# A transformer block on one core: seven-product pairs in all ten groups of the first feed-forward product

## The chip, the cores and the metric

The kernel runs on one core of one Trainium2 chip. The metric is the device time of one execution in microseconds (us). TensorE (PE) multiplies, VectorE (DVE) and ScalarE (ACT) work on tiles, GpSimd (POOL) and SyncE (SP) mostly issue DMA transfers.

## The reference

One block on 256 tokens of width 2048: a gated delta rule branch and a sparse attention branch are gated and merged, then follow layer norm 1 (its result is `x1`), a gated feed-forward layer of inner width 5632, and layer norm 2. The change is in the feed-forward layer, in the gates ahead of it and in how `x1` and the inner activations are kept:

```python
x1 = layer_norm(ALPHA * x + merged @ w_out, ln1_g, ln1_b)
g, u = split(x1 @ w_ffn_in)              # [256, 2048] x [2048, 2 * 5632]
h = silu(g) * u                          # [256, 5632]
out = layer_norm(ALPHA * x1 + h @ w_ffn_out, ln2_g, ln2_b)
```

## The kernel before, in words

**Numbers.** All is fp32. Each operand is split into a high and a low part that PE can multiply at full rate, and a product is three matmuls (`mm3`): high by high, high by low, low by high. Weights come from memory in chunks of 128x1024 (512 KB) on SP's queue; for each, ACT casts `hi` and DVE subtracts `lo` (`chunk`). Tokens are two blocks of 128.

**Pairs.** The large products run over pairs of contraction tiles (256 rows). A *plain pair* (`plain_pair`) is eight products, 24 matmuls of 128x512. A *seven-product pair* (`seven_pair`) gets the same sums from seven products, 21 matmuls, in the manner of Strassen. For it DVE makes sums of weight tiles (`wt`), which are split as well (`thi`, `tlo`), and it needs sums of the left operand, the *forms* (`f_form` for x1; for the inner activations they are written to memory as `d_g` and read back as `gt`). It has a second set of four PSUM banks (`wbank`, as against `bank`), which `sums_chain` adds up after the last such pair. The two sets come from two pools, `acc` and `aux`, of four banks each, which change roles from group to group. The tiles of a pair have names with a prefix by stage: `g_` in the gates, `f_` in the first feed-forward product, none in the second.

**Stages.** Gates (`gate_group` 0 to 3, with the block `wbb` between the first two and the last two and `wba` behind), merge, `wo`, layer norm 1, then the first feed-forward product: group 0 in two plain blocks (`h_chain`), then ten groups of eight pairs (`x_group`, i = 1 to 10), each 512 columns of g and of u. The table `FQ` says which pairs of a group are seven-product ones. After a group, `hidden_chain` makes silu(g) * u, transposes it on PE, splits it into `hH[i]`, `hL[i]` and, where the output product wants forms, writes these to `d_g`. The output product (`group`) has two groups of 22 pairs; pair 2i and 2i+1 read `hH[i]`, `hL[i]`, and `WQ` lists its seven-product pairs.

**Order.** PE and SP follow the program's order as written. DVE, ACT and POOL are ordered by a scheduler with priorities. Side work is written as generators (*chains*), which go on at *ticks*; a tick follows each 12 matmuls (half a pair), and `yield 4` waits four ticks.

**Memory on the chip.** The tiles for `f_wraw`, `f_wt`, `f_thi`, `f_tlo` lie in the places of `hH[7]` to `hH[10]` and `hL[7]` to `hL[10]`, and the forms in the place of `x1`, which is written out to `d_x1` by POOL and read back at i = 8.

Of the kernel before, what the change touches and what calls it, by code (L numbers as in the profile page):

```python
# [34 lines left out]
X1T_WAIT = ((5, 1, 1, 1), (6, 1, 2, 2))  # L35
INV_WAIT = 6
VT_WAIT = 6
WQ = ((2, 4, 6, 8, 9, 11, 13, 14, 16, 18, 19), (3, 5, 7, 8, 10, 12, 13, 15))

GQ = ((4, 6), (2, 4, 6), (2, 4, 6), (2, 4, 6))  # L40
WALL = sorted({*WQ[0], *WQ[1]})
FQ = {1: (4, 6), 2: (4, 6), 3: (3, 4, 6), 4: (4, 6), 5: (3, 4, 6), 6: (4, 6), 7: (3, 4, 6)}

LN2_LOAD = (5, 7, 9, 11)
HELD = 4
N_WARM = 9

# [5 lines left out]
def block_kernel(ctx: ExitStack, tc: tile.TileContext, xT, x, cpack, onehot, relb, convw, alog, dtb, gnw,  # L53
# [13 lines left out]
    def ps_acc():  # L67
        return acc.tile([P, 512], F32, name="acc", tag="acc")
# [20 lines left out]
    def start(gen, at_once=False):  # L89
        chains.append([gen, clock[0] + (next(gen) if at_once else 0)])  # L90
# [20 lines left out]
    def finish():  # L111
        while chains:
            tick()
# [49 lines left out]
            nc.tensor.matmul(ps, xh, lv[:, kk], start=False, stop=False)  # L163
            nc.tensor.matmul(ps, xl, hv[:, kk], start=False, stop=(k == 2 * n - 1))  # L164

    def block_xs(srcs, lh, ll):
        pss = [ps_acc(), ps_acc()]
        for ci, src in enumerate(srcs):
            hi, lo = chunk(src)
            for tb in range(NTB):  # L170
                xs_mm(pss[tb], hi, lo, ci, len(srcs), lh, ll, tb)
            tick()
        return pss
# [262 lines left out]
    def v4(a):  # L436
        return a.rearrange("p (h j) -> p h j", h=4)
# [529 lines left out]
        gate_group(gb, i)  # L967
    for j in range(4):
        js = slice(j * 512, (j + 1) * 512)
        for tb, ps in enumerate(block_xs([wbb[j, k] for k in range(4)], oh_, ol_)):  # L970
            nc.vector.tensor_mul(gb[tb][:, js], ps, gb[tb][:, js])  # L971
    event("bb")
    for i in range(2):
# [21 lines left out]
    hH, hL = [], []

    def h_tiles(pool, n):
        for _ in range(n):
            i = len(hH)
            hH.append(pool.tile([P, 4, S], F32R, name=f"hH{i}", tag=f"hH{i}"))  # L1000
            hL.append(pool.tile([P, 4, S], F32R, name=f"hL{i}", tag=f"hL{i}"))

    h_tiles(hp_, 5)
# [53 lines left out]
    def x1T_chain(tb):  # L1057
        for j in range(4):
            yield X1T_WAIT[tb][j]
            with tc.high_priority(offset=3 * LEAD):  # L1060
                transposed_split(x1, j, tb)
        nc.gpsimd.dma_start(d_x1[tb], x1[tb])
        if tb:
            event("x1")

# [9 lines left out]

    fp = xs_.enter_context(tc.tile_pool(name="fp", bufs=1, side="right", reuse_waits="tile"))

    for tag, shape, dtype, n in (("v", [P, 512], F32, 4), ("hq", [P, 512], F32, 1), ("fg", [P, 2, 4, P], F32, 1),
                                 ("gs", [P, 2, 2, 4, P], F32R, 1)):
        fp.tile(shape, dtype, name=tag, tag=tag, bufs=n)  # L1080

    def fv():
        return fp.tile([P, 512], F32, name="v", tag="v", bufs=4)
# [8 lines left out]
    def h_chain(j, tb, sg, ps):  # L1092
        yield 2
        a = ps()
        for i in range(2):
            nc.tensor.transpose(a[:, i * P:(i + 1) * P], sg[:, i, :], ident)
        ts = slice(tb * P, tb * P + P)
        fs = slice(2 * j, 2 * j + 2)
        split(hH[0][:, fs, ts], hL[0][:, fs, ts], a[:, :2 * P].rearrange("p (k t) -> p k t", k=2))

    block_xs_stag([wfi[0, k] for k in range(8)], xh, xl, ex,
                  lambda tb, ps: start(h_chain(0, tb, gated(tb, ps), ps_aux)))
    l1.close()
# [14 lines left out]

    def f_forms_chain():
        yield "x1"  # L1120
        t = [rp.tile([P, 2, 2, 4, P], F32R, name="f_form", tag=f"x1_{tb}") for tb in range(NTB)]
        for i, q in enumerate((4, 6, 3)):
            yield 1
            f_form[q] = t[i // 2][:, i % 2, 0], t[i // 2][:, i % 2, 1]
            x_form(q, f_form[q], fv(), fv())
# [6 lines left out]

    def hidden_chain(i, bank, v, std):

        if v is None:
            v = [fv() for _ in range(4)]
            for tb in range(NTB):
                nc.scalar.activation(v[2 * tb], bank[2 * tb], AF.Silu)
                nc.vector.tensor_mul(v[2 * tb + 1], bank[2 * tb + 1], v[2 * tb])
        else:  # L1140
            for tb in range(NTB):
                g, u = v[2 * tb:2 * tb + 2]
                nc.vector.tensor_tensor(g, bank[2 * tb], g, op=OP.subtract if tb else OP.add)
                nc.scalar.activation(g, g, AF.Silu)
                nc.vector.tensor_add(u, bank[2 * tb + 1], u)
            for tb in range(NTB):
                g, u = v[2 * tb:2 * tb + 2]
                nc.vector.tensor_mul(u, u, g)
        yield 4 if i < NG else 2
        a = [quad(lambda o, f: nc.tensor.transpose(o, v[2 * tb + 1][:, f * P:(f + 1) * P], ident), std)  # L1150
             for tb in range(NTB)]
        ps = [p for p in (2 * i, 2 * i + 1) if p in WALL]
        if ps:
            hq = fp.tile([P, 512], F32, name="hq", tag="hq", bufs=1)
            nc.scalar.copy(hq, a[1])
        for tb in range(NTB):
            ts = slice(tb * P, tb * P + P)
            split(hH[i][:, :, ts], hL[i][:, :, ts], v4(a[tb]))
        if ps:
            def pv(t, j):  # L1160
                t = t.rearrange("p (q two t) -> p q two t", two=2, t=P)
                return t[:, slice(ps[0] % 2, ps[-1] % 2 + 1), j]
            n = len(ps)
            g = fp.tile([P, 2, 4, P], F32, name="fg", tag="fg", bufs=1)[:, :n]
            gi = [g[:, :, j] for j in range(4)]
            forms(gi, pv(a[0], 0), pv(hq, 0), pv(a[0], 1), pv(hq, 1))
            gs = fp.tile([P, 2, 2, 4, P], F32R, name="gs", tag="gs", bufs=1)[:, :n]
            split(gs[:, :, 0], gs[:, :, 1], g)
            for j, p in enumerate(ps):
                nc.gpsimd.dma_start(d_g[WALL.index(p)], gs[:, j].rearrange("p a b t -> p (a b t)").bitcast(F32))  # L1170

    NG = FT // 4 - 1
    for i in range(1, NG + 1):
        if i > 7:
            h_tiles(hp2, 1)
        if i == 8:
            x1 = [rp.tile([P, D], F32, name=f"x1_{tb}", tag=f"x1_{tb}") for tb in range(NTB)]
            for tb in range(NTB):
                nc.gpsimd.dma_start(x1[tb], d_x1[tb])
        std, shared = (ps_aux, ps_acc) if i % 2 else (ps_acc, ps_aux)  # L1180
        sums = []

        def places():
            sums.extend(fv() for _ in range(4))
            return sums

        bank = x_group(wfg[i - 1], FQ.get(i, ()), std, shared, f_form, fhome, places)
        start(hidden_chain(i, bank, sums or None, std), at_once=True)
    h_tiles(hp2, 1)
    hh_, hl_ = KV(hH), KV(hL)  # L1190


# [147 lines left out]
def _arrays(i):  # L1340
# [13 lines left out]
    def paired(m):  # L1354
# [63 lines left out]
```

## Time and profile before

| | |
|---|---|
| three runs | 1476.67, 1478.28, 1478.88 us |
| median | 1478.28 us |
| profiled execution, its own time | 1477.79 us |
| its span in the profile | 1476.0 us |
| granted PE clock, mean | 0.998 of full |
| busy: PE, DVE, ACT, POOL | 1459.3, 1146.1, 766.5, 52.6 us |

The span goes from the first to the last instruction of the trace; the execution's own time holds what lies around it as well. Busy times are sums over an engine's instructions, so an engine can be busy for 78% of the span and still be the one that is waited for in some stage.

### The profile page before, as it was taken

To read this page: it belongs to the slowest core of one execution; us is meant where nothing else is said; L and a number is where in the kernel's file an instruction comes from. 1 tells how busy PE (TensorE), PEld (TensorE's weight loads), DVE (VectorE), ACT (ScalarE), POOL (GpSimd) and SP (SyncE) were. 2 spreads that over 40 slices of the span, in tenths; PEclk is the share of its full clock that TensorE was granted. 3 is DMA by queue.
4 is the path that set the end of the run, shared out by engine and by line. 5 is a ranking of instruction groups with operands and counts; after the bars stand their busy time and mean duration, and the time that the engine had idled before them with its cause. 6 is when DMAs were issued, how large, how long until landed. Compare 5 with 4: busy or idle time off the path is not lost.

```text
span 1476.0 us, 19311 instructions
## 1 busy us (share of the span) xinstructions
PE 1459.3 (99%) x7191; PEld 1226.0 (83%) x7191; DVE 1146.1 (78%) x1534; ACT 766.5 (52%) x932; POOL 52.6 (4%) x63
## 2 busy tenths in 40 slices
PE   9999999999999999999999999999999999999996
PEld 9888888888888888888878888888888888888885
DVE  6798985468488678776676889988895556999896
ACT  6765443446466456543445556555554444664560
POOL 0001010020010000000000000000000000000000
PEclk9999999999999999999999999999999999999999
DMA  8656584545556665558656566666676666877862
GB/s 295 193 153 198 179 193 152 158 129 158 168 185 215 199 213 187 186 185 299 227 187 207 184 234 216 218 216 236 227 255 220 200 209 224 303 262 244 322 217 87
DMA packets 92398, 307.59 MB, mean 208 GB/s; under 512 B 16448, under 2 KB 17512, under 8 KB 91280
## 3 DMA queue, kind: packets, MB, share of 16 engines
q1 hardware_dynamic: 80592, 283.36, 58.9%
q0 software_dynamic: 4672, 20.65, 4.0%
q10 hardware_dynamic: 7040, 2.36, 0.7%
q8 instruction: 56, 0.92, 0.3%
q14 instruction: 38, 0.31, 0.1%
HBM read 292.50 MB, written 13.83 MB: 208 GB/s over the span
## 4 chain that ended last, share of the span: by engine, by line
PE 95%; DVE 2%; DMA 1%; ACT 1%; issue 1%; SPq 0%; POOLq 0%; DVEq 0%; ACTq 0%
PE acc L142 10%; PE acc L205 10%; PE acc L206 10%; PE acc L204 10%; PE aux L205 8%; PE aux L206 8%; PE aux L204 8%; PE acc L164 7%; PE acc L163 7%; PE acc L162 7%; PE acc L145 5%; PE aux L669 1%; DMA raw<-in_win_dram 1%; DVE lo L82 1%; ACT hi L80 1%
## 5 line engine op out<-in xcount | busy, mean ns | idle before, releaser
L82 DVE TENSOR_TENSOR lo<-raw,hi 128x1024 fp32r<-128x1024 f32 (+1 forms) x421 | 514.8, 1228 | 240.2 <-ACT hi L80 237.1
L80 ACT CAST hi<-raw 128x1024 fp32r<-128x1024 f32 (+1 forms) x421 | 437.7, 1046 | 483.6 <-PE acc L164 125.3
L142 PE MATMUL acc<-X,hi 128*128 128x512 f32 x640 | 203.7, 400 | 0.0
L204 PE MATMUL acc<-hi,X 128*128 128x512 f32 x388 | 151.6, 391 | 0.5 <-DVE s_vT L971 0.5
L206 PE MATMUL acc<-hi,X 128*128 128x512 f32 x388 | 151.0, 389 | 0.0
L205 PE MATMUL acc<-lo,X 128*128 128x512 f32 x388 | 151.0, 389 | 0.0
L145 PEld LDWEIGHTS acc<-X,lo 128*128 128x128 f32 x640 | 120.2, 188 | 28.3
L204 PE MATMUL aux<-hi,X 128*128 128x512 f32 x340 | 132.9, 391 | 0.0
L206 PE MATMUL aux<-hi,X 128*128 128x512 f32 x340 | 132.4, 389 | 0.0
L205 PE MATMUL aux<-lo,X 128*128 128x512 f32 x340 | 132.3, 389 | 0.0
L162 PE MATMUL acc<-hi,X 128*128 128x512 f32 x320 | 127.1, 397 | 0.0
L145 PE MATMUL acc<-X,lo 128*128 128x256 f32 x640 | 126.0, 278 | 0.0
L164 PE MATMUL acc<-hi,X 128*128 128x512 f32 x320 | 124.7, 390 | 0.0
L163 PE MATMUL acc<-lo,X 128*128 128x512 f32 x320 | 124.6, 389 | 0.0
L142 PEld LDWEIGHTS acc<-X,hi 128*128 128x128 f32 x640 | 97.5, 189 | 2.0 <-ACT hi L80 0.7
L204 PEld LDWEIGHTS acc<-hi,X 128*128 128x128 f32 x388 | 72.8, 188 | 15.9 <-DVE s_vT L971 1.0
L206 PEld LDWEIGHTS acc<-hi,X 128*128 128x128 f32 x388 | 72.8, 188 | 15.1
L205 PEld LDWEIGHTS acc<-lo,X 128*128 128x128 f32 x388 | 72.9, 188 | 15.0
L206 PEld LDWEIGHTS aux<-hi,X 128*128 128x128 f32 x340 | 63.8, 188 | 13.3
L205 PEld LDWEIGHTS aux<-lo,X 128*128 128x128 f32 x340 | 63.8, 188 | 13.1
L204 PEld LDWEIGHTS aux<-hi,X 128*128 128x128 f32 x340 | 63.8, 188 | 13.0
L164 PEld LDWEIGHTS acc<-hi,X 128*128 128x128 f32 x320 | 60.1, 188 | 12.7
(518 smaller groups left out, 2562.6 us busy)
## 6 DMA issues: line engine op xcount, KB each, us to landing
raw<-in_wfg_dram SPq DMA_DIRECT2D x143, 512.0 KB, 4.0
raw<-in_wws_dram SPq DMA_DIRECT2D x80, 512.0 KB, 3.8
raw<-in_wfo_dram SPq DMA_DIRECT2D x69, 512.0 KB, 4.6
raw<-in_wgt_dram SPq DMA_DIRECT2D x53, 512.0 KB, 3.6
raw<-in_win_dram SPq DMA_DIRECT2D x37, 512.0 KB, 3.7
raw<-in_wo_dram SPq DMA_DIRECT2D x32, 512.0 KB, 4.3
wraw<-in_wfo_dram SPq DMA_DIRECT2D x19, 512.0 KB, 5.0
gt<-d_g SPq DMA_DIRECT2D x19, 512.0 KB, 6.6
```

Source lines behind the costliest of these rows:

```text
L80: nc.scalar.copy(hi, raw)
L82: nc.vector.tensor_sub(lo, raw, hi.bitcast(F32))
L142: nc.tensor.matmul(pss[c], hv[:, kk, cs[c]], X2[k // 4][:, k % 4], start=(k == 0), stop=False, skip_group_check=True)
L145: nc.tensor.matmul(pss[c][:, :S], lv[:, kk, cs[c]], xh[:, k, :], start=False, stop=(k == KT - 1), skip_group_check=True)
L162: nc.tensor.matmul(ps, xh, hv[:, kk], start=(k == 0), stop=False)
L163: nc.tensor.matmul(ps, xh, lv[:, kk], start=False, stop=False)
L164: nc.tensor.matmul(ps, xl, hv[:, kk], start=False, stop=(k == 2 * n - 1))
L204: nc.tensor.matmul(o, sh, hi, start=first, stop=False)
L205: nc.tensor.matmul(o, sh, lo, start=False, stop=False)
L206: nc.tensor.matmul(o, sl, hi, start=False, stop=last)
L669: nc.tensor.matmul(o, l, r, start=True, stop=True)
```

## The change

- `FQ`: before, groups 1 to 7 had two or three seven-product pairs (17 in all) and 8 to 10 had none. Now group 1 has (4, 6) and the nine others (2, 4, 6), 29 in all.
- `WQ`: 18 instead of 19 seven-product pairs in the output product.
- `hidden_chain`: the transposes come after three ticks in every group (before: four, and two in the last). Both transposed tiles are copied by ACT into `v` tiles (`hq`), and the splits and forms read the copies.
- To free places, the inner activations of group 0 and of groups 1 and 2 go to *passing tiles* (in the place of `hH0`, `hL0`) and are written to memory by POOL (`put_out`, `d_h`). They become positions 8, 9 and 10 of the output product and are read back one by one by SP in its group 0 (`fetch`); the other groups move to positions 0 to 7, and the rows of `w_ffn_out` are reordered on the host to match.
- `x1` is stored by SP, in the program's order, at the start of `f_forms_chain`, two ticks apart, and the forms follow; it is read back by SP in four 512 KB pieces at pairs 15 to 18 of group 0 of the output product.
- The last quarter of `wbb` takes its banks from `aux` instead of `acc`.

```diff
-WQ = ((2, 4, 6, 8, 9, 11, 13, 14, 16, 18, 19), (3, 5, 7, 8, 10, 12, 13, 15))
+WQ = ((2, 4, 6, 8, 9, 11, 12, 16, 17, 19), (3, 5, 7, 8, 10, 12, 13, 16))
-FQ = {1: (4, 6), 2: (4, 6), 3: (3, 4, 6), 4: (4, 6), 5: (3, 4, 6), 6: (4, 6), 7: (3, 4, 6)}
+FQ = ((4, 6), *[(2, 4, 6)] * 9)
+OUT_AT = (8, 9, 10)
+FETCH = (5, 7, 9, 10, 13, 14)
...
-        for tb, ps in enumerate(block_xs([wbb[j, k] for k in range(4)], oh_, ol_)):
+        for tb, ps in enumerate(block_xs([wbb[j, k] for k in range(4)], oh_, ol_, ps_aux if j == 3 else ps_acc)):
...
+    def put_out(i, hl):
+        for j, t in enumerate(hl):
+            nc.gpsimd.dma_start(d_h[i, j], t.rearrange("p k t -> p (k t)").bitcast(F32))
+    def fetch(i, j):
+        t = (hH, hL)[j][i]
+        nc.sync.dma_start(t.rearrange("p k t -> p (k t)").bitcast(F32), d_h[i, j])
...
-        nc.gpsimd.dma_start(d_x1[tb], x1[tb])
...
         yield "x1"
+        for tb in range(NTB):
+            yield 2
+            nc.sync.dma_start(d_x1[tb], x1[tb])
...
-        for i, q in enumerate((4, 6, 3)):
+        for i, q in enumerate((4, 2, 6)):
...
-        yield 4 if i < NG else 2
+        yield 3
...
-        if ps:
-            hq = fp.tile([P, 512], F32, name="hq", tag="hq", bufs=1)
-            nc.scalar.copy(hq, a[1])
+        hq = v[::2]
+        with tc.high_priority(offset=LEAD // 2):
+            for tb in range(NTB):
+                nc.scalar.copy(hq[tb], a[tb])
+        at = OUT_AT[i - 1] if i < 3 else i - 3
...
-            split(hH[i][:, :, ts], hL[i][:, :, ts], v4(a[tb]))
+            split(hl[0][:, :, ts], hl[1][:, :, ts], v4(hq[tb]))
+        if i < 3:
+            put_out(at, hl)
...
-            for tb in range(NTB):
-                nc.gpsimd.dma_start(x1[tb], d_x1[tb])
...
+            if not g and q in FETCH:
+                fetch(OUT_AT[0] + FETCH.index(q) // 2, FETCH.index(q) % 2)
+            if not g and 15 <= q < 19:
+                c, tb = divmod(q - 15, 2)
+                cs = slice(c * 1024, c * 1024 + 1024)
+                nc.sync.dma_start(x1[tb][:, cs], d_x1[tb, :, cs])
```

The first place is a steady group of the first feed-forward product on DVE, around the writing of the forms (`gs`). Before, with pairs (3, 4, 6):

```order
L251 TENSOR_TENSOR f_wt<-f_wt,f_wraw 128x512
L196 TENSOR_TENSOR gs<-fg,gs 128x2x512
L82 TENSOR_TENSOR lo<-raw,hi 128x1024
L238 TENSOR_TENSOR lo<-f_wraw,hi 128x1024
L238 TENSOR_TENSOR lo<-raw,hi 128x512
L252 TENSOR_TENSOR f_wt<-f_wt,raw 128x512
L238 TENSOR_TENSOR f_tlo<-f_wt,f_thi 128x1024 x2
L82 TENSOR_TENSOR lo<-raw,hi 128x1024 x4
```

And of the change, with pairs (2, 4, 6):

```order
L254 TENSOR_TENSOR f_wt<-f_wt,f_wraw 128x512
L240 TENSOR_TENSOR f_tlo<-f_wt,f_thi 128x1024
L198 TENSOR_TENSOR gs<-fg,gs 128x2x512
L240 TENSOR_TENSOR f_tlo<-f_wt,f_thi 128x1024
L84 TENSOR_TENSOR lo<-raw,hi 128x1024 x2
L240 TENSOR_TENSOR lo<-f_wraw,hi 128x1024
L240 TENSOR_TENSOR lo<-raw,hi 128x512
L250 TENSOR_TENSOR f_wt<-f_wraw,raw 128x1024
```

The operations on `f_tlo` of the pair before now stand on either side of `gs`, with the plain `lo` operations behind them.

The second place is the start of the output product on ACT, where the last group's activations are split and its first seven-product pair is made ready. Before:

```order
L1138 ACTIVATE v<-acc 128x512 x2
L80 CAST hi<-raw 128x1024
L195 CAST hH_10448<-acc 128x4x128 x2
L237 CAST hi<-wraw 128x1024
L237 CAST hi<-raw 128x512
L237 CAST thi<-wt 128x1024
```

And of the change:

```order
L82 CAST hi<-raw 128x1024
L1158 ACTIVATE v<-v 128x512
L1169 COPY v<-acc 128x512 x2
L197 CAST hH_10510<-v 128x4x128 x2
L239 CAST hi<-wraw 128x1024
L239 CAST hi<-raw 128x512
L239 CAST thi<-wt 128x1024
```

Two copies stand ahead of the casts of `hH`; what follows is the same.

The third place is SP's queue in group 0 of the output product, in the change; before, these rows have no `d_h`.

```order
L1217 DMA gt<-d_g 128x1024
L1014 DMA hH_10612<-d_h 128x1024
L80 DMA raw<-in_wfo_dram 128x1024 x2
L233 DMA wraw<-in_wfo_dram 128x1024
L235 DMA raw<-in_wfo_dram 128x1024
L1217 DMA gt<-d_g 128x1024
L1014 DMA hL_10613<-d_h 128x1024
L80 DMA raw<-in_wfo_dram 128x1024 x2
```

The fetches of the passing activations stand between the loads of weights and of forms.

## Rows read from the trace of the kernel before

**Rows 1.** The page: PE's busy time; the chain that ended last, by engine.

```profile
PE 1459.3 (99%) x7191; PEld 1226.0 (83%) x7191; DVE 1146.1 (78%) x1534; ACT 766.5 (52%) x932; POOL 52.6 (4%) x63
...
PE 95%; DVE 2%; DMA 1%; ACT 1%; issue 1%; SPq 0%; POOLq 0%; DVEq 0%; ACTq 0%
```

**Rows 2.** Timeline of PE, group 6: start, duration, line, output<-inputs.

```profile
941.06 1.03 PE L1150 MATMUL aux<-ident,v 128*128 128x128 f32 x8
...
942.40 0.39 PE L206 MATMUL acc<-hi,X 128*128 128x512 f32 x1
...
983.66 0.39 PE L205 MATMUL aux<-lo,X 128*128 128x512 f32 x1
...
984.12 1.04 PE L1150 MATMUL acc<-ident,v 128*128 128x128 f32 x8
```

**Rows 3.** Timeline of PE, group 7 with pairs (3, 4, 6).

```profile
997.28 0.39 PE L204 MATMUL acc<-f_thi,f_form 128*128 128x512 f32 x1
997.81 0.50 PE L205 MATMUL acc<-f_tlo,f_form 128*128 128x512 f32 x1
998.14 0.40 PE L206 MATMUL acc<-f_thi,f_form 128*128 128x512 f32 x1
```

**Rows 4.** Timeline, end of `wbb`; in brackets idle time and its releaser.

```profile
533.62 0.39 PE L206 MATMUL acc<-hi,X 128*128 128x512 f32 x1
...
534.56 0.50 PE L204 MATMUL acc<-hi,X 128*128 128x512 f32 x1 [0.55 <-DVE s_vT L971]
...
534.90 0.40 PE L205 MATMUL acc<-lo,X 128*128 128x512 f32 x1
```

**Rows 5.** Timeline of DVE, group 7, around the wait of rows 3.

```profile
996.54 2.35 DVE L238 TENSOR_TENSOR f_tlo<-f_wt,f_thi 128x1024 fp32r<-128x1024 f32 x2
998.81 1.22 DVE L238 TENSOR_TENSOR lo<-f_wraw,hi 128x1024 fp32r<-128x1024 f32 x1
999.94 0.68 DVE L238 TENSOR_TENSOR lo<-raw,hi 128x512 fp32r<-128x512 f32 x1
1000.54 1.22 DVE L248 TENSOR_TENSOR f_wt<-f_wraw,raw 128x1024 f32<-128x1024 f32 x1
```

**Rows 6.** Timelines of ACT, DVE and PE, start of the output product.

```profile
1241.39 1.08 ACT L195 CAST hH<-acc 128x512 fp32r<-128x512 f32 x2 [4.83 <-PE acc L1150]
...
1242.01 1.29 DVE L196 TENSOR_TENSOR hL<-acc,hH 128x512 fp32r<-128x512 f32 x2 [4.19 <-ACT hH L195]
...
1249.88 1.23 DVE L238 TENSOR_TENSOR tlo<-wt,thi 128x1024 fp32r<-128x1024 f32 x1
...
1240.76 1.04 PE L1150 MATMUL acc<-ident,v 128*128 128x128 f32 x8
...
1250.52 0.39 PE L204 MATMUL acc<-thi,gt 128*128 128x512 f32 x1
1251.16 0.50 PE L205 MATMUL acc<-tlo,gt 128*128 128x512 f32 x1 [0.25 <-DVE tlo L238]
```

**Rows 7.** Windows, group 5: PE, PEld, DVE, ACT, POOL busy, clock, DMA share, GB/s.

```profile
887.50:930.50 43.00, 42.85 (x193) 35.21 (x193) 41.38 (x49) 25.69 (x31) 1.06 (x2) 1.00 0.64 209
```

**Rows 8.** Timeline of ACT, group 6, the copy before.

```profile
942.39 0.58 ACT L1155 COPY hq<-aux 128x512 f32<-128x512 f32 x1
942.87 1.07 ACT L195 CAST hH<-aux 128x512 fp32r<-128x512 f32 x2
```

**Rows 9.** Timeline of PE, group 1, the first use of a form of x1.

```profile
824.56 0.39 PE L204 MATMUL aux<-hi,f_form 128*128 128x512 f32 x1
```

**Rows 10.** Windows, group 0 of the output product and after: columns of rows 7.

```profile
1240.00:1296.00 56.00, 55.75 (x251) 45.88 (x250) 53.50 (x57) 34.57 (x39) 0.00 (x0) 1.00 0.86 302
1296.00:1332.00 36.00, 36.00 (x161) 29.80 (x160) 34.62 (x37) 20.86 (x23) 0.00 (x0) 1.00 0.67 230
...
1370.00:1382.00 12.00, 12.00 (x54) 9.94 (x54) 10.28 (x12) 6.73 (x7) 1.06 (x2) 1.00 1.00 374
```

**Rows 11.** Timeline of DVE, group 6 with two seven-product pairs.

```profile
964.36 1.22 DVE L82 TENSOR_TENSOR lo<-raw,hi 128x1024 fp32r<-128x1024 f32 x1 [1.50 <-ACT hi L80]
```

More of the change, by code (lines that the diff above doesn't have):

```diff
@@ L164, in xs_mm, with block_xs @@
             nc.tensor.matmul(ps, xl, hv[:, kk], start=False, stop=(k == 2 * n - 1))
-    def block_xs(srcs, lh, ll):
-        pss = [ps_acc(), ps_acc()]
+    def block_xs(srcs, lh, ll, ps=ps_acc):
+        pss = [ps(), ps()]
         for ci, src in enumerate(srcs):
@@ L994, in block_kernel, with h_tile, passing @@
     hp_ = fh.enter_context(tc.tile_pool(name="hp", bufs=1, side="left", reuse_waits="tile"))
[L995 to L1003, printed above, removed]
+    hH, hL = [None] * (FT // 4), [None] * (FT // 4)
+    def h_tile(pool, i):
+        hH[i], hL[i] = (pool.tile([P, 4, S], F32R, name=f"{hl}{i}", tag=f"{hl}{i}") for hl in ("hH", "hL"))
+    d_h = dr.tile([FT // 4, 2, P, 1024], F32, name="d_h")
+    def passing():
+        return [hp_.tile([P, 4, S], F32R, name="pass", tag=f"{hl}0") for hl in ("hH", "hL")]
+    def put_out(i, hl):
[4 more added lines that the diff above has]
+        nc.sync.dma_start(t.rearrange("p k t -> p (k t)").bitcast(F32), d_h[i, j])
+    h_first = passing()
+    for i in range(1, 5):
+        h_tile(hp_, i)
     l1 = ExitStack()
@@ L1076, in block_kernel @@
     fp = xs_.enter_context(tc.tile_pool(name="fp", bufs=1, side="right", reuse_waits="tile"))
-    for tag, shape, dtype, n in (("v", [P, 512], F32, 4), ("hq", [P, 512], F32, 1), ("fg", [P, 2, 4, P], F32, 1),
+    for tag, shape, dtype, n in (("v", [P, 512], F32, 4), ("fg", [P, 2, 4, P], F32, 1),
                                  ("gs", [P, 2, 2, 4, P], F32R, 1)):
@@ L1098, in h_chain @@
         fs = slice(2 * j, 2 * j + 2)
-        split(hH[0][:, fs, ts], hL[0][:, fs, ts], a[:, :2 * P].rearrange("p (k t) -> p k t", k=2))
+        split(h_first[0][:, fs, ts], h_first[1][:, fs, ts], a[:, :2 * P].rearrange("p (k t) -> p k t", k=2))
+        if j and tb:
+            put_out(OUT_AT[2], h_first)
     block_xs_stag([wfi[0, k] for k in range(8)], xh, xl, ex,
@@ L1104, in block_kernel @@
     hp2 = fh.enter_context(tc.tile_pool(name="hp2", bufs=1, side="left", reuse_waits="tile"))
-    h_tiles(hp2, 2)
+    for i in (5, 6):
+        h_tile(hp2, i)
     f_home = {}
@@ L1133, in hidden_chain @@
     def hidden_chain(i, bank, v, std):
-        if v is None:
-            v = [fv() for _ in range(4)]
-            for tb in range(NTB):
[L1138 to L1148, printed above, removed]
-        yield 4 if i < NG else 2
+        for tb in range(NTB):
+            g, u = v[2 * tb:2 * tb + 2]
+            nc.vector.tensor_tensor(g, bank[2 * tb], g, op=OP.subtract if tb else OP.add)
+            nc.scalar.activation(g, g, AF.Silu)
+            nc.vector.tensor_add(u, bank[2 * tb + 1], u)
+        for tb in range(NTB):
+            g, u = v[2 * tb:2 * tb + 2]
+            nc.vector.tensor_mul(u, u, g)
+        yield 3
         a = [quad(lambda o, f: nc.tensor.transpose(o, v[2 * tb + 1][:, f * P:(f + 1) * P], ident), std)
              for tb in range(NTB)]
-        ps = [p for p in (2 * i, 2 * i + 1) if p in WALL]
-        if ps:
-            hq = fp.tile([P, 512], F32, name="hq", tag="hq", bufs=1)
-            nc.scalar.copy(hq, a[1])
+        hq = v[::2]
+        with tc.high_priority(offset=LEAD // 2):
+            for tb in range(NTB):
+                nc.scalar.copy(hq[tb], a[tb])
+        at = OUT_AT[i - 1] if i < 3 else i - 3
+        if i == 3:
+            h_tile(hp_, 0)
+        hl = passing() if i < 3 else (hH[at], hL[at])
         for tb in range(NTB):
             ts = slice(tb * P, tb * P + P)
-            split(hH[i][:, :, ts], hL[i][:, :, ts], v4(a[tb]))
+            split(hl[0][:, :, ts], hl[1][:, :, ts], v4(hq[tb]))
+        if i < 3:
+            put_out(at, hl)
+        ps = [p for p in (2 * at, 2 * at + 1) if p in WALL]
         if ps:
@@ L1165, in hidden_chain @@
             gi = [g[:, :, j] for j in range(4)]
-            forms(gi, pv(a[0], 0), pv(hq, 0), pv(a[0], 1), pv(hq, 1))
+            forms(gi, pv(hq[0], 0), pv(hq[1], 0), pv(hq[0], 1), pv(hq[1], 1))
             gs = fp.tile([P, 2, 2, 4, P], F32R, name="gs", tag="gs", bufs=1)[:, :n]
@@ L1173, in block_kernel @@
     for i in range(1, NG + 1):
[L1174 to L1178, printed above, removed]
-                nc.gpsimd.dma_start(x1[tb], d_x1[tb])
         std, shared = (ps_aux, ps_acc) if i % 2 else (ps_acc, ps_aux)
@@ L1185, in places @@
             return sums
-        bank = x_group(wfg[i - 1], FQ.get(i, ()), std, shared, f_form, fhome, places)
-        start(hidden_chain(i, bank, sums or None, std), at_once=True)
-    h_tiles(hp2, 1)
+        bank = x_group(wfg[i - 1], FQ[i - 1], std, shared, f_form, fhome, places)
+        if i == NG:
+            h_tile(hp2, 7)
+        start(hidden_chain(i, bank, sums, std), at_once=True)
     hh_, hl_ = KV(hH), KV(hL)
@@ L1245, in group @@
                 finish()
+                for i in OUT_AT:
+                    h_tile(hp2, i)
+                for tb in range(NTB):
+                    x1[tb] = rp.tile([P, D], F32, name=f"x1_{tb}", tag=f"x1_{tb}")
                 xs_.close()
@@ L1393, in _arrays @@
         "wfg": paired(wf1),
-        "wfo": paired(np.asarray(i["w_ffn_out"])[0]),
+        "wfo": paired(np.asarray(i["w_ffn_out"])[0].reshape(FT // 4, 512, D)[[*range(3, FT // 4), 1, 2, 0]].reshape(D_FF, D)),
         "ln1g": ca(np.asarray(i["ln1_g"])[0]),
```

## The prediction, on record before the change was run

> **What bounds the kernel now.** The page comes first: TensorE (PE) is busy 1459.3 us, 99% of the span, and the chain that ended last is PE for 95% of it [rows 1]. So the time is the number of matmuls times their pitch, plus the places where PE waits. The pitch comes from PE's timeline: between the transposes of two groups of the first feed-forward product, 182 matmuls of 128x512 follow the one at 942.40 without a gap, up to 983.66: 41.26 / 182 = 0.2267 us each [rows 2]. A plain pair (24 of them) is 5.44 us, a seven-product pair (21) 4.76. From transposes to transposes that two-seven group of 186 matmuls lasts 984.12 - 941.06 = 43.06 us, so the eight transposes take 0.89.
>
> The waits show in the same timeline as larger steps between starts. In each group with three seven-product pairs (there are three such groups) one step is 0.53 and the next 0.33 instead of 0.227: 0.41 us lost together [rows 3]. The multiplication by `wbb` hands its banks to the next gates group late: 0.94 + 0.34 - 2 x 0.227 = 0.83 lost [rows 4]. At the first seven-product pair of the output product a step is 0.64, 0.41 lost [rows 6].
>
> Second comes VectorE (DVE), the engine that could take over. Back to back its pitch is 1.13 us for a 128x1024 operation and 0.60 for 128x512 [rows 5]. A plain pair costs it two of the former, 2.26; a seven-product pair four of 1024 and three of 512, 6.32. In the window of a three-seven group it is busy 41.38 us of 43, with PE at 42.85 [rows 7].
>
> **The change part by part.**
>
> *Matmuls.* The ten groups go from 17 sevens to 29, the output product from 19 to 18: 11 more sevens, each three matmuls fewer. 33 x 0.2267 = **-7.48 us**, if PE stays the bound.
>
> *Which pairs.* With (3, 4, 6), pairs 3 and 4 stand side by side; DVE meets both, a `gs` and two plain `lo` in one stretch, and the `f_tlo` operations from 996.54 on are what PE waits for until 997.81 [rows 3, 5]. With (2, 4, 6) a plain pair lies between any two, and in the order the `f_tlo` of pair 4 no longer stands behind `gs` and two plain `lo`. I laid the new order of DVE and ScalarE (ACT) for one group out at these pitches: every tile is ready 2.3 us or more before PE asks, and DVE idles about 1 us per group. So the three waits go, 3 x 0.41 = **-1.23**, and none comes in their place. The other bound is that each of nine groups loses 0.41 as those three did: +2.5 instead. I take the former, by the laid-out order.
>
> *`wbb` in the other pool.* Its last quarter takes its banks from the pool that the next group does not accumulate in. The matmul that waited until 534.56 finds free banks: **-0.83** (0 if another wait, such as that for the first weights of the gates group, ends last there).
>
> *Hidden chain inside the groups.* The transposes come 12 matmuls earlier, two ACT copies (0.48 each, from the start of one to the next operation [rows 8]) replace one or none, and the splits read those copies. The copies free the banks for the next seven-product accumulators, now opened at pair 2; in my layout they end 11.3 us after the group's start, and PE wants the banks at 13.9. **0**; if that cover were gone, up to 0.5 per group.
>
> *Start of the output product.* This is what gets worse. Before, the last group's transposes come after 24 matmuls, at 1240.76; ACT casts `hH` from 1241.39 on and `wraw` behind it; DVE, at 1242.01, has idled 4.19 us for this `hH`, and behind `hL` stand the seven steps of the first seven-product pair, down to the `tlo` of 1249.88 that PE waits for at 1251.16 [rows 6]. Now the last group waits one tick more, 12 x 0.2267 = 2.72 us, and two copies stand ahead of the casts, 2 x 0.48 = 0.96. All that is behind starts 3.68 us later, and as PE waits already, it is paid in full: **+3.7**. Bounds: 2.7 if the copies are hidden, 4.7 if a release of tiles slips too. Queued behind it are the tiles of pairs 3 and 4, which keep their distance to PE.
>
> *Forms of x1.* The two stores of x1 move to SP's queue, and the forms start four ticks (10.9 us) later. PE's first matmul with a form stands at 824.56 [rows 9], after the four plain pairs (21.8 us) with which group 1 begins, and the forms were made before that group began: **0**. Each 1 MB store now stands ahead of weight loads; at the fullest rate seen, 374 GB/s [rows 10], that is 2.8 us, against some 7 us by which loads run ahead there: 0, at most 1.
>
> *Hidden tiles through memory, x1 in pieces.* In group 0 of the output product SP now issues six fetches and four pieces of x1, 0.524 MB each, between weight loads, and one `gt` less. From 1240 to 1332 us, 302 GB/s x 56 us + 230 x 36 = 25.2 MB were moved [rows 10]; now 29.9 MB in about 92.5 us, 323 GB/s. In the first 56 us alone, with five of the fetches, it is 349. The fullest stretch shows 374, so it fits: **0**. At the 302 of that stretch the 29.9 MB take 99.0 us, 6.5 too long; but it was only 86% full. I take 0, since even its fullest part needs less than 374, and keep 6.5 as the other end.
>
> In these rows weights and `gt` come by SP's one queue, and no row has x1 in it. The Trainium skill (DMA: Bandwidth & Descriptors, section Queues, rings and completion order) speaks against the move: on each DMA engine the ring of one queue row is consumed in order, while different rows are served in turn. So x1, which on POOL's row shared the engines with weights, would on SP's stand whole ahead of them. By the rule a piece holds up the loads behind it for its full time, and the sum would lose up to what rival (b) prices, where by the rows it loses nothing; no run here shows that yet.
>
> *Sum*: -7.48 - 1.23 - 0.83 + 3.7 = -5.8. The profiled execution took 1477.79 us, so 1472.0; the median of the runs, 1478.28, lies 0.49 above it: **1472.5**.
>
> **Rivals.**
>
> (a) *The late transposes cost nothing*, since ACT and DVE catch up while plain pairs run: without the +3.7, 1468.8. Against it: PE already waits at 1251.16, at the end of a row of steps that each wait for the one before [rows 6]. Chance 0.09.
>
> (b) *Transfers*: the ten added loads stand whole in front of weights, and group 0 loses between 0 and 6.5 us; half of that is 1475.7. For it: 349 GB/s are wanted where 302 went at 86% [rows 10], which is 351 if full. Against: 374 is reached later on, and PE's later start leaves the first loads 3.7 us more. It decides once the stretch can't move what PE's pace wants. Chance 0.20.
>
> (c) The other side: *DVE becomes the bound of the three-seven groups*. It is busy 41.38 us in such a group [rows 7], and PE's new period is 183 x 0.2267 + 0.89 = 42.4. In a two-seven group DVE idles up to 1.50 us in front of a single `lo` while ACT is behind [rows 11]. If 2.2 us of such idling can't be avoided, a group lasts 43.6, 1.2 too long; nine groups cost 11, 1483.5. It decides where the idling passes 42.4 - 41.4 = 1.0. Against it: the groups with three sevens keep PE's pace now but for the one wait, at the same work per pair. Chance 0.11.
>
> **How the numbers follow.** The forecast has the remaining 0.60, with its own range from 1471 to 1474. The three runs of before lie 0.15% apart, so about 0.2%, 3.0 us, can be told from no change: faster is below 1475.3, slower above 1481.2. The forecast and (a) are faster; (b) is so in a third of its cases and else the same; (c) is slower in nine of ten. Faster 0.75, same 0.15, slower 0.10. The range goes from just under (a), 1468.5, to 1477.5, well into (b); beyond it lie most of (c) and the worst of (b), about 0.15, and the lowest cases of (a).
>
> **What would show it.** PE has 33 matmuls fewer, but for records that are missing. A group of (2, 4, 6) lasts 42.4 us from transposes to transposes, with no step over 0.35 apart from these; 43 or more is (c), with DVE almost never idle. Around the `wbb` banks there is no step. At the first seven-product pair of the output product PE loses about 4.1 us in all, and the last release there is a `tlo`; nothing lost there is (a). In pairs 5 to 19 of group 0 PE keeps its pitch; lost time there, with DVE or ACT waiting for `raw`, `wraw` or `gt` to land, is (b). The forecast would fail most quietly if each of the nine equal groups lost a little: 0.3 us each is 2.7 in all.

## The result and the profile after

The changed kernel takes 1470.75 us (median of 4 runs, 1468.79 to 1471.24) against 1477.91 of the kernel before in the same comparison: a ratio of 0.995, 95% interval 0.9932 to 0.9967, so 5 to 10 us less. The forecast was 1472.5, faster, in a range of 1468.5 to 1477.5. The profiled execution took 1471.15 us, with a span of 1469.3.

The page of the changed kernel, with the rows that answer to [rows 1]; the third is the chain that ended last:

```profile
span 1469.3 us, 19377 instructions
...
PE 1452.5 (99%) x7158; PEld 1220.3 (83%) x7158; DVE 1200.8 (82%) x1608; ACT 789.5 (54%) x970; POOL 52.5 (4%) x63
...
PE 95%; DVE 2%; DMA 2%; issue 0%; ACT 0%; SPq 0%; POOLq 0%; DVEq 0%; ACTq 0%
```

PE has 33 matmuls fewer (7191 to 7158 in the records) and is 6.8 us less busy; DVE, which pays for them, is 54.7 us more busy, and PE is still 99% busy.

Where the time went is read from PE's timeline: the same matmul is looked up in both traces, and the difference of its starts followed through the program.

| place | before | after | difference | step |
|---|---|---|---|---|
| after the first loads | 143.08 | 143.67 | +0.59 | +0.59 |
| first matmul after `wbb` | 534.56 | 534.45 | -0.11 | -0.70 |
| 15 us later, in the gates group | 549.02 | 549.55 | +0.53 | +0.64 |
| end of layer norm 1 | 767.05 | 766.71 | -0.34 | -0.87 |
| first seven-product pair of the output product | 1247.12 | 1237.35 | -9.77 | -9.43 |
| its last `tlo` step | 1251.16 | 1245.04 | -6.12 | +3.65 |
| end of group 0 there | 1333.34 | 1328.28 | -5.06 | +1.06 |
| last matmul | 1463.32 | 1457.93 | -5.39 | -0.33 |
| end of the span | 1476.0 | 1469.3 | -6.7 | -1.3 |

Of the +1.06, 0.68 are the three matmuls that the output product has more; 0.29 is a gap at pair 17, of which more below. The first row is scatter: that matmul starts between 142.55 and 144.11 us in the thirteen traces of this document.

The ten groups are as forecast. Windows of three of the groups with (2, 4, 6), from transposes to transposes (columns as in [rows 7]):

```profile
893.65:936.00 42.35, 42.35 (x193) 35.13 (x192) 39.69 (x49) 26.07 (x32) 1.59 (x3) 1.00 0.69 236
936.00:978.40 42.40, 42.40 (x193) 35.21 (x192) 38.44 (x44) 25.18 (x30) 0.00 (x0) 1.00 0.59 199
...
1063.98:1106.37 42.39, 42.39 (x192) 35.19 (x191) 40.98 (x49) 26.28 (x31) 1.05 (x2) 1.00 0.65 224
```

PE is busy throughout, 42.4 us as worked out, and DVE idles 1.4 to 4.0 us. At the start of the output product, timelines of ACT, DVE and PE of the changed kernel, as [rows 6]:

```profile
1234.23 1.07 ACT L1169 COPY v<-acc 128x512 f32<-128x512 f32 x2 [7.00 <-PE acc L1164]
1235.19 1.15 ACT L197 CAST hH<-v 128x512 fp32r<-128x512 f32 x2
...
1235.86 1.29 DVE L198 TENSOR_TENSOR hL<-v,hH 128x512 fp32r<-128x512 f32 x2 [6.11 <-ACT hH L197]
1237.33 1.23 DVE L240 TENSOR_TENSOR lo<-wraw,hi 128x1024 fp32r<-128x1024 f32 x1 [0.18 <-ACT hi L239]
...
1233.55 1.04 PE L1164 MATMUL acc<-ident,v 128*128 128x128 f32 x8
...
1238.61 0.50 PE L207 MATMUL acc<-lo,hH 128*128 128x512 f32 x1 [0.77 <-DVE lo L240]
...
1242.09 0.50 PE L207 MATMUL acc<-tlo,gt 128*128 128x512 f32 x1 [0.76 <-DVE tlo L240]
...
1243.78 0.50 PE L206 MATMUL acc<-thi,gt 128*128 128x512 f32 x1 [0.26 <-ACT thi L239]
1245.04 0.50 PE L207 MATMUL acc<-tlo,gt 128*128 128x512 f32 x1 [0.76 <-DVE tlo L240]
```

DVE idles 6.11 us for `hH` where it had 4.19; PE now waits for a `lo`, then for a `tlo`, then for ACT's `thi` and the second `tlo`. Adding up all steps over 0.227 us there, PE loses 4.26 us, against 0.52 before.

### The profile page after: what moved, and what is told of

Its sections match the earlier page's. It is cut to its first block, busy times and chain, and to the rows that moved or that the text cites. A ratio compares the mean times of both kernels' runs of the same rounds, so it can differ in the third digit from the quotient of the medians.

```text
span 1469.3 us, 19377 instructions
## 1 busy us (share of the span) xinstructions
PE 1452.5 (99%) x7158; PEld 1220.3 (83%) x7158; DVE 1200.8 (82%) x1608; ACT 789.5 (54%) x970; POOL 52.5 (4%) x63
## 4 chain that ended last, share of the span: by engine, by line
PE 95%; DVE 2%; DMA 2%; issue 0%; ACT 0%; SPq 0%; POOLq 0%; DVEq 0%; ACTq 0%
PE acc L144 10%; PE acc L207 9%; PE acc L208 9%; PE acc L206 9%; PE aux L206 9%; PE aux L207 9%; PE aux L208 9%; PE acc L166 7%; PE acc L164 7%; PE acc L165 7%; PE acc L147 5%; PE aux L671 1%; DMA raw<-in_win_dram 1%; DVE lo L84 1%; PE aux L946 0%
## 5 line engine op out<-in xcount | busy, mean ns | idle before, releaser
L84 DVE TENSOR_TENSOR lo<-raw,hi 128x1024 fp32r<-128x1024 f32 (+1 forms) x399 | 486.7, 1229 | 179.6 <-ACT hi L82 176.5
L82 ACT CAST hi<-raw 128x1024 fp32r<-128x1024 f32 (+1 forms) x399 | 414.0, 1045 | 397.0 <-PE acc L166 121.7
L206 PE MATMUL aux<-hi,X 128*128 128x512 f32 x328 | 128.2, 391 | 0.3 <-DVE ol__105 L198 0.3
L206 PE MATMUL acc<-hi,X 128*128 128x512 f32 x328 | 128.1, 391 | 0.0
L208 PE MATMUL aux<-hi,X 128*128 128x512 f32 x328 | 127.7, 389 | 0.0
L208 PE MATMUL acc<-hi,X 128*128 128x512 f32 x328 | 127.7, 389 | 0.0
L207 PE MATMUL acc<-lo,X 128*128 128x512 f32 x328 | 127.6, 389 | 0.0
L207 PE MATMUL aux<-lo,X 128*128 128x512 f32 x328 | 127.6, 389 | 0.0
L164 PE MATMUL acc<-hi,X 128*128 128x512 f32 x320 | 127.1, 397 | 0.0
L166 PE MATMUL acc<-hi,X 128*128 128x512 f32 x320 | 124.7, 390 | 0.0
L165 PE MATMUL acc<-lo,X 128*128 128x512 f32 x320 | 124.6, 389 | 0.0
L239 ACT CAST f_thi<-f_wt 128x1024 fp32r<-128x1024 f32 x58 | 61.1, 1054 | 43.0 <-DVE f_wt L250 24.6
L240 DVE TENSOR_TENSOR f_tlo<-f_wt,f_thi 128x1024 fp32r<-128x1024 f32 x58 | 70.6, 1221 | 2.0 <-ACT f_thi L239 1.4
L208 PEld LDWEIGHTS acc<-hi,X 128*128 128x128 f32 x328 | 61.6, 188 | 12.8
L207 PEld LDWEIGHTS acc<-lo,X 128*128 128x128 f32 x328 | 61.6, 188 | 12.6
```

Of the source, the lines that this page charges most:

```text
L82: nc.scalar.copy(hi, raw)
L84: nc.vector.tensor_sub(lo, raw, hi.bitcast(F32))
L164: nc.tensor.matmul(ps, xh, hv[:, kk], start=(k == 0), stop=False)
L206: nc.tensor.matmul(o, sh, hi, start=first, stop=False)
L207: nc.tensor.matmul(o, sh, lo, start=False, stop=False)
L208: nc.tensor.matmul(o, sl, hi, start=False, stop=last)
```

## The experiments

Seven alter the changed kernel in one place, three build on the first of these, and one is the kernel before again. Times are medians; the kernel before gave 1477.9 to 1478.5 in each of the comparisons.

**The last group as before.** Two ticks and no copies in the last group alone.

```diff
-        yield 3
+        yield 3 if i < NG else 2
...
-        hq = v[::2]
-        with tc.high_priority(offset=LEAD // 2):
-            for tb in range(NTB):
-                nc.scalar.copy(hq[tb], a[tb])
+        hq = v[::2] if i < NG else a
+        if i < NG:
+            with tc.high_priority(offset=LEAD // 2):
+                for tb in range(NTB):
+                    nc.scalar.copy(hq[tb], a[tb])
```

> The changed kernel, but in the last group alone the transposes come after two ticks and the splits read PSUM without copies, as before. My theory: the 4.26 us that PE now loses around the first seven-product pair of the output product come from the 2.72 + 0.96 us by which the transposed activations are late; the loss falls to about 0.5 us and the time by 3.7 us, to about 1467. Rival, transfers: the loss comes from weights or forms of that pair that land late behind the fetches; then it stays near 4.3 us and the time near 1470.8.

1466.61 us (1465.78 to 1467.2, 5 runs), 0.9921 of before, 0.9909 to 0.9934: 4.1 below the changed kernel. In PE's timeline of this kernel one wait is left at that pair:

```profile
1239.09 0.39 PE L206 MATMUL acc<-thi,gt 128*128 128x512 f32 x1
1239.73 0.50 PE L207 MATMUL acc<-tlo,gt 128*128 128x512 f32 x1 [0.25 <-DVE tlo L240]
```

With the step behind it that is 0.52 us, as before the change. The transfers were untouched, so it is not they that delay this pair.

**The tick alone.** The copies kept (`yield 3 if i < NG else 2` and nothing else).

> The changed kernel with the transposes of the last group after two ticks, and the copies kept. My theory adds the two parts of the delay: of the 3.7 us between the changed kernel (PE loses 4.26 us at the first seven-product pair) and e1_last_early (0.51) the tick is 2.72 and the copies 0.96, so PE loses about 1.5 here. Rival: one of the two alone decides, the later of tick and copies; then it is 0.5 or 4.3.

One execution, 1467.95 us. PE loses 0.41 us ahead of the second of these rows of its timeline, 1.04 behind it and 0.11 at the step after, 1.56 in all:

```profile
1240.00 0.40 PE L208 MATMUL acc<-thi,gt 128*128 128x512 f32 x1
1240.64 0.50 PE L206 MATMUL acc<-thi,gt 128*128 128x512 f32 x1 [0.25 <-ACT thi L239]
```

So the tick was worth 4.26 - 1.56 = 2.70 and the copies 1.56 - 0.52 = 1.04: the two add up, as the sum had them (2.72 and 0.96).

**`wbb` in the old pool.**

```diff
-        for tb, ps in enumerate(block_xs([wbb[j, k] for k in range(4)], oh_, ol_, ps_aux if j == 3 else ps_acc)):
+        for tb, ps in enumerate(block_xs([wbb[j, k] for k in range(4)], oh_, ol_)):
```

> The changed kernel with the last quarter of wbb in the pool acc again. The prediction's term: PE waits 0.83 us at the end of wbb again, and the time rises by 0.8 us. Rival, from the traces of before and after: PE was in step with before 15 us later, since a 0.35 us wait for ol__105 and two smaller ones came in its place; then the wait at the end of wbb returns, those go, and 15 us later PE stands where it does in the changed kernel, within 0.15 us: no change in time.

1471.19 us (1470.75 to 1471.75), which can't be told from 1470.75; the times do not decide between 0 and 0.83. Against the changed kernel's trace its matmuls stand at +0.43 us after the first loads, +1.31 behind `wbb` and +0.71 15 us later: 0.88 lost, 0.60 of it given back. The gain of the new pool is 0.3 us here, and 0.06 in the table above. What takes it back is seen in PE's timeline of the changed kernel:

```profile
546.28 0.50 PE L206 MATMUL aux<-hi,X 128*128 128x512 f32 x1 [0.35 <-DVE ol__105 L198]
```

But that wait belongs to this one execution. The same two places in PE's timeline of the first experiment's kernel, whose engines run the same instructions in the same order up to here:

```profile
543.77 1.03 PE L850 MATMUL aux<-ident,s_mn 128*128 128x128 f32 x8
544.56 0.50 PE L206 MATMUL aux<-hi,X 128*128 128x512 f32 x1
```

From the matmul ahead of the wait of [rows 4] to the one at 549.55 the changed kernel takes 15.33 us, the nine other traces with the new pool 14.74 to 15.02, and the three with the old pool 15.39 to 15.60. So the new pool gains 0.4 to 0.9 us in nine of ten traces, 0.75 by the medians, and the trace in the table is the exception.

**Pairs 3 and 4 side by side.**

```diff
-FQ = ((4, 6), *[(2, 4, 6)] * 9)
+FQ = ((4, 6), *[(3, 4, 6)] * 9)
...
-        for i, q in enumerate((4, 2, 6)):
+        for i, q in enumerate((4, 3, 6)):
```

> The changed kernel with (3, 4, 6) in place of (2, 4, 6) in the nine groups; the count of matmuls is the same. The prediction's step: two seven-product pairs side by side make PE wait for f_tlo, 0.41 us in each group as in the three groups of before, nine times, 3.7 us in all. Rival: the three waits of before came from the place of gs and hq in DVE's order, which the copies into SBUF changed as well; then PE has no gap in the groups and the time is the same.

1472.61 us (1472.4 to 1473.29), 1.9 above. All of PE's steps over 0.227 in the groups, other than at the transposes, add up to 2.75 us where the changed kernel has none; the two largest, in PE's timeline:

```profile
1080.47 0.50 PE L207 MATMUL acc<-f_tlo,f_form 128*128 128x512 f32 x1 [0.30 <-DVE f_tlo L240]
...
1209.15 0.50 PE L207 MATMUL aux<-f_tlo,f_form 128*128 128x512 f32 x1 [0.82 <-DVE f_tlo L240]
```

Adjacent pairs do make PE wait for `f_tlo`, 0.31 us per group on average (none in two groups, 0.2 to 0.3 in five, 0.57 and 1.08 in these two) and not 0.41 in each. The copies are no cure for it.

**Six fetches more.** The same tiles a second time, at pairs 3 to 8.

```diff
+            if not g and 3 <= q < 9:
+                fetch(OUT_AT[0] + (q - 3) // 2, (q - 3) % 2)
```

> The changed kernel with six more fetches of 0.524 MB on SP in pairs 3 to 8 of group 0 of the output product, the same tiles a second time. My theory: transfers have room there; in these pairs about 348 GB/s are wanted now and 400 with them, above the 374 seen at the fullest, so that of the 3.1 MB only what doesn't fit delays PE: 0 to 3 us. Rival (b) of the prediction, each transfer holds up the weights behind it by its whole time: 6 x 1.4 = 8.4 us more, and 10 x 1.4 = 14 us would go if the ten present ones were gone, which the sum does not leave room for; 1.4 us each or nearly is expected by it here.

1473.40 us (1472.88 to 1474.56), 2.65 above. Windows of group 0 of the output product, the changed kernel first:

```profile
1233.00:1289.00 56.00, 53.38 (x234) 42.46 (x233) 51.34 (x55) 32.93 (x38) 0.00 (x0) 1.00 0.85 314
1289.00:1326.00 37.00, 36.97 (x163) 30.29 (x162) 30.48 (x32) 19.07 (x21) 0.00 (x0) 1.00 0.81 300
```

And with six fetches more:

```profile
1233.00:1289.00 56.00, 51.89 (x224) 40.60 (x223) 48.48 (x52) 31.80 (x37) 0.00 (x0) 1.00 0.92 356
```

The DMA goes from 314 to 356 GB/s, 0.92 full, and PE then has three waits for `tlo`, two at pair 9 and one at pair 12, 2.5 us with the step behind each. The median landing time of `raw` from 1233 to 1330 us goes from 5.4 to 6.1 us. The transfers alone would be 8.4 us at 374 GB/s; so most of it fits in. The six fetches of the changed kernel lie in pairs 5 to 14, where its PE has no gap.

**x1 read back by POOL.** Two pieces of 1 MB at pairs 15 and 16.

```diff
-            if not g and 15 <= q < 19:
-                c, tb = divmod(q - 15, 2)
-                cs = slice(c * 1024, c * 1024 + 1024)
-                nc.sync.dma_start(x1[tb][:, cs], d_x1[tb, :, cs])
+            if not g and q in (15, 16):
+                nc.gpsimd.dma_start(x1[q - 15], d_x1[q - 15])
```

> The changed kernel with x1 read back by POOL in two pieces of 1 MB at pairs 15 and 16 in place of SP's four of 0.5 MB at 15 to 18. My theory: x1 on SP costs nothing, since PE has one small gap (0.29 us) from pair 5 to pair 21 there; the time stays within 0.5 us, and the gap stays, since it is at two adjacent seven-product pairs, 16 and 17. Rival, rivals of the prediction (b): x1 whole ahead of the weights is what makes that gap; it goes, and weights land sooner than the 5.4 (raw) and 6.4 us (wraw) of the changed kernel.

1469.94 us (1469.24 to 1470.24), which can't be told from the changed kernel. But the one gap that PE has in pairs 5 to 21 of the changed kernel,

```profile
1321.15 0.39 PE L206 MATMUL acc<-thi,gt 128*128 128x512 f32 x1
1321.57 0.50 PE L207 MATMUL acc<-tlo,gt 128*128 128x512 f32 x1
```

is gone. It stands, with 0.29 to 0.31 us, in all nine traces with x1 on SP, and in neither of the two with x1 on POOL; so it came from the way in which x1 is read back and not from pairs 16 and 17 being adjacent alone, as I had put it. The `wraw` of pair 17 lands 9.4 us after its issue in the changed kernel and 7.8 in this one. By the rule of the Trainium skill that the prediction names (DMA: Bandwidth & Descriptors, section Queues, rings and completion order: each ring is consumed in its own order), x1 on SP's queue would hold up the weights behind it; the traces agree in the sign, and the size is 0.29 us. The edit changes the size and the time of the pieces along with the queue, so that the queue alone does it is likely, not shown.

**Three sevens in group 1 too**, on top of the last group as before.

```diff
-FQ = ((4, 6), *[(2, 4, 6)] * 9)
+FQ = ((2, 4, 6),) * 10
...
-        for i, q in enumerate((4, 2, 6)):
+        for i, q in enumerate((2, 4, 6)):
```

> The kernel of e1_last_early, and group 1 with the pairs (2, 4, 6) too, with the forms made in the order 2, 4, 6. My theory: three matmuls fewer are 0.68 us less, if the form of pair 2 is there in time: the copy of e1_last_early at 1466.6 goes to 1465.9. Rival: the forms start four ticks later since x1 is stored by SP first, and the form of pair 2, wanted 11 us after the group's start rather than 22, is late; then PE waits in pair 2 of group 1 for 1 us or more, and the time is that of e1_last_early or above.

1472.99 us (1471.16 to 1474.47): 6.4 us lost for three matmuls fewer. The rival's time, but not its cause: the form was written in time, and PE waited for a bank. PE's timeline of this kernel, in group 1:

```profile
814.39 0.39 PE L208 MATMUL acc<-f_thi,f_form 128*128 128x512 f32 x1
818.60 0.77 PE L206 MATMUL acc<-f_thi,f_form 128*128 128x512 f32 x1 [3.82 <-DVE pass L198]
819.16 0.63 PE L207 MATMUL acc<-f_tlo,f_form 128*128 128x512 f32 x1
819.59 0.63 PE L208 MATMUL acc<-f_thi,f_form 128*128 128x512 f32 x1
```

The bank still holds the last transposed activations of group 0, until DVE's `pass` operation at 818.04, which in DVE's order stands behind steps for pair 4 while pair 2 waits:

```profile
817.44 0.68 DVE L240 TENSOR_TENSOR lo<-raw,hi 128x512 fp32r<-128x512 f32 x1
818.04 0.41 DVE L198 TENSOR_TENSOR pass<-acc,pass 128x256 fp32r<-128x256 f32 x1
```

The loss is 3.98 us there and 2.8 after it, of which more below.

**One pair more in the output product**, on top of that: pair 17 of its second group.

```diff
-WQ = ((2, 4, 6, 8, 9, 11, 12, 16, 17, 19), (3, 5, 7, 8, 10, 12, 13, 16))
+WQ = ((2, 4, 6, 8, 9, 11, 12, 16, 17, 19), (3, 5, 7, 8, 10, 12, 13, 16, 17))
```

> The kernel of e8_ten_alike, and pair 17 of the second group of the output product as a seven-product pair behind 16, 19 in all there as before. By the count of matmuls 0.68 us less. Rival, from the three gaps of pairs side by side: 16 and 17 are adjacent and DVE is late with tlo, 0.3 us or more, and the held last pairs start with DVE behind; then half or all of the 0.68 is lost.

1475.28 us (1473.93 to 1476.47), 2.3 above the kernel that it is built on. The held last pairs start late: PE's timeline,

```profile
1436.32 0.39 PE L208 MATMUL acc<-thi,hL 128*128 128x512 f32 x1
1437.65 0.50 PE L206 MATMUL acc<-hi,hH 128*128 128x512 f32 x1 [0.94 <-ACT hi L82]
```

and five waits there, this one and four for DVE's `lo`, lose 4.1 us. That ACT's four `hi` casts come only behind the last seven-product pair is seen; that they wait for its tiles, whose place they take, is argued from the code.

**All that helped together.** The kernel of the first experiment, x1 on POOL, and (3, 4, 6) in group 1, whose second accumulators open one pair later.

```diff
-FQ = ((4, 6), *[(2, 4, 6)] * 9)
+FQ = ((3, 4, 6), *[(2, 4, 6)] * 9)
...
-        for i, q in enumerate((4, 2, 6)):
+        for i, q in enumerate((3, 4, 6, 2)):
```

> The kernel of e1_last_early with x1 read back by POOL as in e5_x1_pool, and group 1 with (3, 4, 6) in place of (4, 6). My theory: the gap of 0.29 us at pair 17 goes as in e5_x1_pool; a third seven-product pair saves 0.68 and, since the second accumulators open at pair 3, 5.4 us later than in e8_ten_alike, the 4.1 us wait for the bank that the activations of group 0 still hold does not come back, less 0.4 at most for the adjacent pairs 3 and 4: about 0.6 below e1_last_early (1466.6), 1466.0. Rival: the bank is still held or the form of pair 3 late; PE waits at pair 3 of group 1, and the time is above 1466.6.

1466.67 us (1464.83 to 1467.88), 0.9921 of before, 0.9908 to 0.9935: the same as the first experiment. In the traces the gain is there: against that kernel its matmuls go from +0.30 us ahead of group 1 to -0.24 behind it (0.54 of the 0.68 that three matmuls are worth; one step there is 0.11 too long) and to -0.53 behind pair 17. It is too small for these runs.

**Four seven-product pairs in nine groups.**

```diff
-FQ = ((4, 6), *[(2, 4, 6)] * 9)
+FQ = ((5, 6), *[(2, 3, 5, 6)] * 9)
...
-        for i, q in enumerate((4, 2, 6)):
+        for i, q in enumerate((5, 6, 2, 3)):
```

> The changed kernel with four seven-product pairs (2, 3, 5, 6) in the nine groups, 27 matmuls fewer in all. It shows how near the prediction's rival (c) is. DVE is busy 38.4 to 39.7 us in the changed kernel's groups and a fourth pair costs it 4.1 us more, 42.5 to 43.8, where PE needs 180 x 0.2267 + 0.89 = 41.7. My theory: DVE is the bound then, a group lasts 43 to 44 us, and the time goes up by 6 to 14 us, to 1477 to 1485. Rival: DVE's busy time in the windows counts overlaps, and the pitch by my count leaves room; then groups last 41.7 and the time falls by 6 us to 1465.

One execution, 1511.09 us. My theory had the direction and much too small a size. A group now lasts 47.6 us; its window:

```profile
1084.80:1132.40 47.60, 44.68 (x189) 35.44 (x188) 44.78 (x54) 28.14 (x33) 1.05 (x2) 0.96 0.58 199
```

DVE is busy 44.78 us of it, 1 us more than the most I had added up, and idles 2.8 all the same; and the granted clock is 0.96. Of the 5.9 us above PE's own 41.7, waits for `f_tlo` and `f_thi` are 4.2 and the lower clock 1.6 (last section). Here two and two pairs stand side by side, which alone made PE wait in the kernel with (3, 4, 6); four pairs spread out were not tried.

**The kernel before, again**, unchanged.

> The kernel before, profiled a second time, unchanged. From the last matmul to the end of the span it took 12.7 us in the first profile, and 11.1 to 11.5 in the profiles of the changed kernel and of nine others; the step from matmul to transpose at the end of layer norm 1 lost 0.95 us, and 0.15 to 0.44 in those. If these belong to one execution, the second profile shows 11.1 to 11.5 and 0.2 to 0.4; if they belong to the kernel before, it shows 12.7 and 0.95 again, and the change moved them.

1478.35 us. From the last matmul (1463.98) to the end of the span (1476.5) it is 12.5 us again, and the step at the end of layer norm 1 loses 0.83. Both belong to the kernel before, and the change moved them.

## Why the prediction was right

**The sum's method held**: pitch times matmuls, plus PE's waits. Matmuls and waits in the ten groups: 12 pairs more there, 36 x 0.2267 = 8.16, and 1.23 for the three waits, are 9.39; the table has 9.43, so the stores of x1 and the later forms cost nothing. That (2, 4, 6) has no wait was shown against (3, 4, 6), whose waits came back, though at 0.31 rather than 0.41 us each.

**The late transposes** were forecast at +3.7 and cost 3.65. That they were the cause, and that their two parts add, was shown by taking both away, and one.

**`wbb`**: "the matmul that waited until 534.56 finds free banks: -0.83". It does. Some of it is given back within 15 us: 0.75 us in the changed kernel's own trace, where PE then waits for `ol__105`, and 0.15 to 0.4 in the nine others. Read from the table the term is 0.06; from all thirteen traces it is about 0.75, near the forecast. The prediction had named another wait as the way in which it could fail, but took no part of it off.

**Transfers through memory** were taken as 0 and cost 0.29, at pair 17. The mechanism of rival (b) is there at a tenth of its price, 3.25: with 3.1 MB more, at 0.92 full, PE lost 2.5.

**Rival (c)** was closer than its chance looks from the result: DVE idles 1.4 to 4.0 us in the three windows above, and with 4.1 us of work more the group passes PE's pace by 5.9 us (47.6 against 41.7), 4.2 of it in waits for DVE and ACT.

**Not foreseen** were two gains of the size of the error. At the end of layer norm 1, ahead of the first transposes of the second token block, PE waits 0.15 to 0.44 us in the eleven changed kernels where it waited 0.83 and 0.95. In DVE's timeline before, a `lo` stands between the two steps that make that piece of x1:

```profile
762.38 0.74 DVE L1029 SCALAR_TENSOR_TENSOR x<-x,mv,lng 128x512 f32<-128x512 f32 x1
763.04 1.22 DVE L82 TENSOR_TENSOR lo<-raw,hi 128x1024 fp32r<-128x1024 f32 x1
764.18 0.74 DVE L1034 SCALAR_TENSOR_TENSOR x<-x,rs,lnb 128x512 f32<-128x512 f32 x1
```

In the changed kernel it no longer does:

```profile
762.68 1.40 DVE L1044 SCALAR_TENSOR_TENSOR x<-x,mv,lng 128x512 f32<-128x512 f32 x2
764.01 1.41 DVE L1049 SCALAR_TENSOR_TENSOR x<-x,rs,lnb 128x512 f32<-128x512 f32 x2
```

It goes with the change, and not with the pool of `wbb`, since the kernel with `wbb` in the old pool has it too; which other part moves that `lo` in the scheduler's order was not tried. And the end of the kernel is 1.3 us shorter (last section). With them, PE's -5.4 and the end's -1.3 make the 6.7 us of the two profiled executions; the medians, 7.2 apart, are within what these runs scatter. That the total came so near is in part luck: these gains, 2.1 us in the table, were met by 0.8 that the table's `wbb` fell short, 0.6 of scatter at the first loads and 0.3 of transfers.

## What to carry to other kernels

When a side chain gets later by a tick, look at the one place where nothing follows to cover it: here nine groups hid the new copies and the last one paid for them in full. A wait that is taken away is worth only what the next wait behind it allows, and that wait can differ from one execution to the next: read a term of less than 1 us from several traces before it is called right or wrong. And DVE, at 91 to 97% of the period here, had no room for one more seven-product pair as it was placed, since part of its idle time was not for use.

## What the runs showed of the hardware that was not expected

**A wait of 4 us cost 2.8 us more after it.** In the kernel with ten groups alike, PE resumed at 818.60 with a pitch of 0.427 us in place of 0.227, for 14 matmuls: 14 x 0.2 = 2.8. Windows of that stretch, the granted clock third from the end:

```profile
806.00:812.00 6.00, 6.00 (x30) 4.99 (x29) 6.00 (x10) 2.62 (x5) 0.58 (x1) 1.00 0.56 178
812.00:818.50 6.50, 2.78 (x13) 1.97 (x11) 6.50 (x11) 3.98 (x5) 0.00 (x0) 0.95 0.90 299
818.50:824.30 5.80, 5.70 (x14) 4.47 (x15) 3.96 (x4) 1.04 (x1) 0.53 (x1) 0.50 0.73 236
824.30:830.00 5.70, 5.70 (x26) 4.73 (x25) 2.58 (x4) 2.23 (x3) 0.00 (x0) 0.97 0.14 27
```

The clock was granted at 0.50, the lower level of 1.2 GHz, and came back some 6 us later. The 4.26 us that the changed kernel loses in several waits, none above 1.03, left it at 1.00:

```profile
1237.00:1246.00 9.00, 6.38 (x22) 3.58 (x21) 8.82 (x10) 6.14 (x8) 0.00 (x0) 1.00 0.43 155
```

In the kernel with four pairs per group, seven of nine waits of 2.0 us had such a stretch behind them, 7 or 8 matmuls at 0.427 us and some 1.6 us lost each, and two had none. That is 11 of the 40 us by which that kernel is slower. PE's timeline and window of one:

```profile
1115.90 0.50 PE L207 MATMUL acc<-f_tlo,f_form 128*128 128x512 f32 x1 [1.76 <-DVE f_tlo L240]
...
1117.20:1120.60 3.40, 3.40 (x10) 2.60 (x9) 2.76 (x4) 0.06 (x1) 0.00 (x0) 0.52 0.93 359
```

**The last output transfer is 1 us longer in the kernel before.** Its last transfer on SP lands after 3.1 us, in both profiles of it (3.1 and 3.0); in the eleven changed kernels after 2.0 to 2.1. DMA of the last 5 us, kernel before:

```profile
q14 instruction: 1, 0.01, 0.4%
...
out_dram<-x SPq DMA_DIRECT2D x1, 256.0 KB, 3.1
```

And changed:

```profile
out_dram<-x SPq DMA_DIRECT2D x1, 256.0 KB, 2.1
```

In both profiles of the kernel before, a packet of the instruction queue falls into those 5 us; in the other eleven none does. That it is this packet that holds up the end is likely, not shown.
